# Another issue order for the mixers and the context feed-forward, and two more weight buffers for the small experts

## The chip, the cores and the metric

The kernel runs on one core of a Trainium2 chip. A core has a matrix engine (TensorE, PE in the rows), VectorE (DVE), ScalarE (ACT), GpSimd (POOL) and SyncE (SP), each with an instruction queue of its own that runs in order, and 16 DMA engines that serve the queues of all of them. The metric is the device time of one execution in microseconds, as the median of the runs.

## What is computed

Two transformer blocks stand one behind the other, on 256 tokens of width 1024, in float32. The first has two layers: a mixer (pooling, a gated convolution and spatial gating) and a feed-forward, which is dense in layer 0 and a mixture of experts in layer 1.

```python
for l in range(DEPTH):                                 # first block, DEPTH = 2
    mod = silu(c) @ ada_w[l] + ada_b[l]                # shift, scale and gate, two of each
    x = x + gate_m * (mixer1(rms_norm(x) * (1 + scale_m) + shift_m) @ w_out[l])
    h = rms_norm(x) * (1 + scale_f) + shift_f
    y = swiglu(h, ...) if l == 0 else moe_swiglu(h, ...)   # top 2 of 8 experts, hidden 3584
    x = x + gate_f * y
x = rms_norm(x, final_norm_g)
```

The second block takes this x and a context of 256 tokens. In its layer 0 the context goes through a mixer (a gated recurrence, differential attention, a Fourier mix) and a feed-forward of its own; neither needs x. In layer 1 only the context's keys and states are needed.

```python
for l in range(DEPTH):                                 # second block
    yl, yc = mixer(hl, hc, ...)                        # x also looks at the context's keys, states
    xl = xl + ml[2] * rms_norm_2(yl, g[1])
    xl = xl + ml[5] * rms_norm_2(swiglu_2(adaln(xl, ...), w_ffn_in[l], w_ffn_out[l]), g[3])
    if l < DEPTH - 1:                                  # the context stream, layer 0
        xc = xc + mc[2] * rms_norm_2(yc, g[1])
        xc = xc + mc[5] * rms_norm_2(swiglu_2(adaln(xc, ...), w_ffn_in[l], w_ffn_out[l]), g[3])
```

## The kernel before

Weights come in tiles of 128x1024 float32 (0.5 MB) by DMAs that SP issues (`wload`, line 213). In most layers each weight tile is split into a rounded part (ScalarE, line 320) and the remainder (VectorE, line 321), and each product is made of three matmuls (`mm3`, lines 236, 241 and 242). The small experts (the four with at most 64 tokens each) take the weights unsplit instead: a step loads four tiles and issues 16 products (`burst`, lines 260 and 264). The four large experts work as the other layers do.

The work is written as Python generators. A `Task` wraps one with a `Res`, the set of buffer pools that it takes its tiles from, and a key. A key is a priority class: `use` (line 135) sets the priority counter that each traced instruction gets, and the classes start at 0 (lead), one million (fill), two million (tail) and three million (late). When the kernel is built, a planner goes through the traced instructions with a timeline of its own, and puts on each engine, of the instructions that it takes to be ready, the one with the lowest number. So a lower class fills what a higher one leaves free; what is planned then runs in order on each engine.

`plan` (from line 1220) sets the classes. In the first block, `block1_mix` and `block1_ffn` of layer 0 and `block1_mix` of layer 1 are lead on resources R0 (tiles w0, h0, accumulators a0, t0). The context stream B with the modulation vectors G1 and G2 is fill on R1 (w1, w2, h1, h2, accumulators a1, t1, t2); for its feed-forward B goes to RF, which has three w1 and two h1 buffers, thus one split weight tile at a time. `block1_out` of layer 1 and `moe` are tail.

B runs as fill up to "normed", the point ahead of its feed-forward. That has 66 loads and as many steps, one load each: a gate/up step has 24 matmuls of 256 columns, a down step 12 of 512. Three of them are late. Then `moe` goes a step (normalization, router, and a branch at line 909 that only an overflow of the experts takes, which every engine reads a register for) and a second one (rows of the first expert). After it `turns` takes a's (expert steps) and b's (context steps) by a pattern; `issue_after` ties the first matmul of each to the last of the other before it. A small expert has 21 steps, so there are 84. When the small experts are through ("alone"), `moe` changes to RN, which also has the w1, w2, h1 and h2 buffers, and to a class below all others.

The weights of an expert are addressed by its number, which comes out of the routing, so no expert load can be issued before that. At its end the context stream adds a gate row that GpSimd loads (`gate_bc`, line 1318), multiplied in by VectorE at line 1344. In the small experts' resources RS, the weight tiles come in turn from w0 (four buffers) and h0 (four buffers).

Of the kernel before, what the change touches and what calls it, by code (L numbers as in the profile page):

```python
# [26 lines left out]
LEVELS = [64, 32, 16, 8, 4, 2, 1]  # L27
N_EXP = 8
LB_LAYER = 1
WEAVE = ("rardy" * 9, "r" + "arrdy" * 9)  # L30
W_BUFS, H_BUFS, S_BUFS = (4, 3, 1), (4, 2, 1), (12, 21, 6, 8)
K_BUFS, G_BUFS, M_BUFS, A_BUFS, T_BUFS = (4, 3), (3, 3), (8, 5), (2, 2), (2, 1, 1)
# [31 lines left out]
class Res:  # L64


    def __init__(self, w, h, a, aw, e, sc, t, s, st, sa, sb, k, g, m):
        self.w, self.h, self.a, self.aw, self.e, self.sc, self.t = w, h, a, aw, e, sc, t
        self.s, self.st, self.sa, self.sb, self.k, self.g, self.m = s, st, sa, sb, k, g, m
        self.sl = st  # L70
        self.i = {}
# [25 lines left out]
class Builder:  # L97
    def __init__(self, tc, A, out, es, taps=None):
        self.tc, self.nc, self.A, self.out = tc, tc.nc, A, out
        self.taps = taps or {}  # L100
        E = es.enter_context

        def pool(name, bufs, **kw):
            return E(tc.tile_pool(name=name, bufs=bufs, **kw))
        self.cp = pool("cp", 1)
        self.xp = pool("xp", 8)
        self.dp = pool("dp", 1, space=bass.MemoryType.DRAM)
        w = [pool(f"w{i}", n) for i, n in enumerate(W_BUFS)]
        h = [pool(f"h{i}", n) for i, n in enumerate(H_BUFS)]
        sp = [pool(f"s{i}", n) for i, n in enumerate(S_BUFS)]  # L110
        k = [pool(f"k{i}", n) for i, n in enumerate(K_BUFS)]
        g = [pool(f"g{i}", n) for i, n in enumerate(G_BUFS)]
        m = [pool(f"m{i}", n) for i, n in enumerate(M_BUFS)]
        a = [pool(f"a{i}", n, space=bass.MemoryType.PSUM) for i, n in enumerate(A_BUFS)]
        pt = [pool(f"t{i}", n, space=bass.MemoryType.PSUM) for i, n in enumerate(T_BUFS)]
        a0, a1, t0, t1, t2 = [a[0]], [a[1]], [pt[0]], [pt[1]], [pt[2]]
        s0, s1, s2, s3 = sp
        wl, hl = [w[0], w[1]] * 3 + [w[0], w[2]], [h[0], h[1]] * 2 + [h[0], h[2], h[0]]
        w1, h1, hm = [w[1]] * 3 + [w[2]], [h[1]] * 2 + [h[2]], [h[0], h[0], w[2]] + [h[0], h[0], h[2]]
        self.R0 = Res(w[:1], h[:1], a0, a0, a0, a0, t0, s0, s0, s2, s0, k[0], g[0], m[0])  # L120
        self.R1 = Res(w1, h1, a1, a1, a1, a1, t1 + t2, s1, s3, s1, s1, k[1], g[1], m[1])
        self.RF = Res(w[1:2], h[1:2], a1, a1, a1, a1, t1, s1, s1, s1, s1, k[1], g[1], m[1])
        self.RS = Res([w[0], h[0]], h[:1], t0, a0, a0, a0, t2 + a0, s3, s2, s2, s3, k[0], g[0], m[0])
        self.RM = Res(w[:1], hm, t0, a0, a0, a0, t2, s3, s2, s2, s3, k[0], g[0], m[0])
        self.RN = Res(wl, hl, t0 + a1, a0, a0, a0, t2 + t1, s3, s2, s2, s3, k[0], g[0], m[0])
        self.RL = Res(wl, hl, a0, a0 + a1, a1, t1 + t2, t0, s1, s0, s2, s3, k[0], g[0], m[0])
        self.R1.sl = s1
        self.xpools = [s0, s1]
        self.R = self.R0
        self.n = 0  # L130
        self.mark = None
        self.key = None
        self.prio = {"lead": 0, "fill": 1000000, "tail": 2000000, "late": 3000000}
# [1086 lines left out]
    def plan(self, xs, m, m2, sh, task, G0, G1, G2, G3):  # L1220
        R0, R1, RL = self.R0, self.R1, self.RL

        def weave(t, *others, label="end"):

            while t.at != label and t.step() != label:
                for o, n in others:
                    o.step(n)

        G0.step(4)
        G0.res = R0  # L1230
        G2.step(4)
        self.use(R1, "fill")
        self.levels_setup()
        if LB_LAYER == 1:
            self.lower_bounds()
        B = task(self.ctx_stream(m2, sh), R1, "fill")
        for _ in range(8):
            B.step()
            G2.step()
        weave(B, (G2, 1), (G1, 1), label="ffn")  # L1240
        G1.run()
        G2.run()
        B.res = self.RF

        weave(task(self.block1_mix(xs, m[0], 0), R0), (G0, 1))
        G0.run()
        task(self.block1_out(xs, m[0], 0), R0).run()
        task(self.block1_ffn(xs, m[0]), R0).run()
        task(self.block1_mix(xs, m[1], 1), R0).run()
        task(self.block1_out(xs, m[1], 1), R0, "tail").run()  # L1250
        moe = task(self.moe(xs, m[1]), self.RS, "tail")
        B.run("normed")
        B.key = "late"
        B.step(3)
        moe.step()
        moe.key = B.key = "tail"
        moe.step()
        self.turns(moe, B, "bbbbb" + "abaab" * 200)
        assert B.at == "end" and moe.at == "alone"
        self.prio["lead"] = 4000000  # L1260
        moe.key = "lead"
        moe.res = self.RN
        moe.run()
        self.use(RL, "lead")
        self.first_end(xs)
        self.tapx("x1", xs)
        self.tapx("xc", self.xc)
        L0 = task(self.lat_stream(xs, m2[0], 0, sh[0]), RL)
        weave(L0, (G3, 1), label="mixed")
        G3.run()  # L1270
        C = task(self.ctx_keys(m2, sh), R1)
        L0.run("ffn")
        L0.res = R0
        weave(L0, (C, 1))
        C.run()
        self.use(RL, "lead")
        self.tapx("xl0", xs)
        L1 = task(self.lat_stream(xs, m2[1], 1, sh[1]), RL)
        L1.run()
# [126 lines left out]
    def mixer2(self, l, H, sh, M, kind):  # L1406
# [77 lines left out]
        def ev_z(d):  # L1484
            lb = []

            def ev(t, ps):
                if l == LB_LAYER and t == 0:
                    lb.append(self.st(512))
                    self.late(nc.gpsimd.dma_start(lb[0], self.lb_rows[d:d + 1].to_broadcast([P, 512])))  # L1490
                    om = self.st(512)
                    S.activation(om, lb[0], AF.Copy, scale=-1.0, bias=1.0)
                    lb.append(om)
                k, f = self.st(512), self.s2(512, pool=self.R.sl)
                S.activation(k, ps, AF.Sigmoid, scale=-1.0)
                S.activation(f, ps, AF.Sigmoid)
                if lb:
                    V.tensor_mul(k, k, lb[1])
                    V.tensor_mul(f, f, lb[1])
                    V.scalar_tensor_tensor(f, f, 2.0 ** -64, lb[0], op0=ALU.max, op1=ALU.add)  # L1500
                    logs.append((f, None))
                else:
                    z = self.st(512)
                    V.tensor_scalar(z, ps, 0.0, None, op0=ALU.min)
                    V.tensor_tensor(f, f, k, op=ALU.min)
                    logs.append((f, z))
                lf[d].append(f)
                kt[d].append(k)
                if full:
                    pk = self.transpose4(k, 4)  # L1510
                    y = self.s2(4, 128)
                    S.copy(y, pk)
                    kT[d].append(y)
# [61 lines left out]
        if lat:  # L1575
# [15 lines left out]
            out = None  # L1591
            for c in WEAVE[l]:
                if c == "a":
# [478 lines left out]
```

## Time and profile before

| | us |
|---|---|
| median of 3 runs | 2841.42 |
| lowest and highest | 2837.86, 2845.29 |
| the profiled execution, its own time | 2833.26 |
| its span | 2831.5 |

| engine | busy us | share of the span |
|---|---|---|
| PE | 2620.4 | 93% |
| DVE | 1594.2 | 56% |
| ACT | 1323.8 | 47% |
| POOL | 104.7 | 4% |

Matmuls are pipelined, so a busy PE need not be a PE at its peak; an idle one is time in which no matmul was under way. The DMA share is the mean busy share of the 16 engines. A row of the timeline has the start, the duration, engine, line, operation, written and read tiles and the count; in brackets, the idle time of the engine before it and what ended it.

### The profile page before, as it was taken

The numbers are of one execution on the slowest core, as the hardware profiler recorded it, in microseconds if no ns is written. First come the engines' busy times: TensorE is split into PE (matmuls) and PEld (weight loads), VectorE is DVE, ScalarE is ACT, GpSimd is POOL, SyncE is SP. The second block draws the span as 40 slices with busy tenths as digits, with TensorE's granted clock in tenths as the row PEclk, the third lists the DMA queues.
The fourth block names the chain that finished last, engine by engine and source line by source line (L and its number), as shares of the span: only waits on it lengthen the run. The fifth ranks groups of instructions, "written<-read, shape, count | busy, mean of one in ns | idle before, by whom it ended". The sixth has DMA issues, their size and how long they took to land.

```text
span 2831.5 us, 44132 instructions
## 1 busy us (share of the span) xinstructions
PE 2620.4 (93%) x16414; PEld 1984.8 (70%) x16414; DVE 1594.2 (56%) x2691; ACT 1323.8 (47%) x1908; POOL 104.7 (4%) x166
## 2 busy tenths in 40 slices
PE   7899999998789899998899999989999999899898
PEld 5667888786654444444588787867768888677897
DVE  3436565665621222122699899985666556666555
ACT  3435445645322111111477777765545644554443
POOL 0010000010100000000000000000000000000000
PEclk8999999999899999999999999999999999899999
DMA  9987766643479999999799999986455556224463
GB/s 359 335 282 252 239 228 223 223 121 116 124 272 372 358 372 365 382 366 377 262 382 357 358 356 361 354 318 214 159 174 162 175 175 197 91 69 142 149 187 110
DMA packets 204383, 716.03 MB, mean 253 GB/s; under 512 B 24858, under 2 KB 29082, under 8 KB 204160
## 3 DMA queue, kind: packets, MB, share of 16 engines
q1 hardware_dynamic: 196112, 692.82, 69.8%
q0 software_dynamic: 7760, 19.75, 2.3%
q8 instruction: 131, 2.15, 0.3%
q14 instruction: 92, 0.75, 0.1%
q10 hardware_dynamic: 288, 0.55, 0.1%
HBM read 707.90 MB, written 5.13 MB: 252 GB/s over the span
## 4 chain that ended last, share of the span: by engine, by line
PE 55%; DMA 9%; DVE 3%; ACT 3%; issue 2%; SPq 0%; POOL 0%; DVEq 0%; ACTq 0%; POOLq 0%
PE a0t L236 7%; PE a0t L241 6%; PE a0t L242 6%; DMA h0t<-in_mgu_dram 6%; PE a1t L236 5%; PE a1t L241 5%; PE a1t L242 5%; PE t0t L264 4%; PE t0t L241 2%; PE t0t L242 2%; PE t0t L236 2%; PE t0t L260 2%; PE a0t L264 1%; PE a1t L1705 1%; DVE h0t L321 1%
## 5 line engine op out<-in xcount | busy, mean ns | idle before, releaser
L320 ACT CAST h0t<-w0t 128x1024 fp32r<-128x1024 f32 (+1 forms) x316 | 327.7, 1038 | 303.8 <-PE a0t L241 222.9
L321 DVE TENSOR_TENSOR h0t<-w0t,h0t 128x1024 fp32r<-128x1024 f32 (+1 forms) x214 | 257.2, 1203 | 230.0 <-ACT h0t L320 217.7
L320 ACT CAST h1t<-w1t 128x1024 fp32r<-128x1024 f32 x144 | 151.0, 1048 | 268.4 <-PE a1t L241 224.3
L236 PE MATMUL a0t<-s0t,h0t 128*128 128x256 f32 x800 | 226.6, 288 | 5.9 <-ACT h0t L320 2.9
L241 PE MATMUL a0t<-s0t,h0t 128*128 128x256 f32 x800 | 224.6, 284 | 0.0
L242 PE MATMUL a0t<-s0t,h0t 128*128 128x256 f32 x800 | 220.0, 286 | 0.2 <-DVE h0t L321 0.2
L321 DVE TENSOR_TENSOR h1t<-w1t,h1t 128x1024 fp32r<-128x1024 f32 x80 | 97.9, 1223 | 211.3 <-ACT h1t L320 207.1
L264 PE MATMUL t0t<-h0t,s0t 128*64 128x512 f32 x448 | 214.7, 625 | 0.0
L236 PEld LDWEIGHTS a0t<-s0t,h0t 128*128 128x128 f32 x800 | 153.0, 192 | 15.3 <-ACT h0t L320 4.6
L264 PE MATMUL t0t<-w0t,s0t 128*64 128x512 f32 x336 | 161.2, 618 | 0.0
L241 PEld LDWEIGHTS a0t<-s0t,h0t 128*128 128x128 f32 x800 | 153.7, 192 | 1.7 <-issue 1.1
L242 PEld LDWEIGHTS a0t<-s0t,h0t 128*128 128x128 f32 x800 | 150.1, 192 | 3.7 <-DVE h0t L321 1.7
L241 PE MATMUL a0t<-h0t,s2t 128*128 128x512 f32 x352 | 139.6, 397 | 0.0
L320 ACT CAST h0t<-w1t 128x1024 fp32r<-128x1024 f32 x101 | 106.1, 1051 | 45.4 <-PE a1t L242 17.1
L236 PE MATMUL a1t<-s1t,h1t 128*128 128x256 f32 x408 | 120.2, 298 | 5.4 <-ACT h1t L320 5.2
L242 PE MATMUL a0t<-h0t,s2t 128*128 128x512 f32 x308 | 120.0, 392 | 0.0
L264 PEld LDWEIGHTS t0t<-w0t,s0t 128*64 128x64 f32 x336 | 48.3, 144 | 99.6 <-issue 99.6
L241 PE MATMUL a1t<-s1t,h1t 128*128 128x256 f32 x408 | 116.0, 287 | 0.0
L236 PE MATMUL a0t<-h0t,s2t 128*128 128x512 f32 x308 | 113.0, 400 | 1.2 <-DVE s0t L1368 0.8
L242 PE MATMUL a1t<-s1t,h1t 128*128 128x256 f32 x396 | 110.6, 290 | 3.1 <-DVE h1t L321 3.1
L260 PE MATMUL t0t<-w0t,s0t 128*64 128x512 f32 x112 | 62.4, 640 | 46.8 <-DMA h0t<-in_mgu_dram 37.1
L236 PEld LDWEIGHTS a1t<-s1t,h1t 128*128 128x128 f32 x408 | 79.3, 195 | 36.3 <-issue 29.6
(804 smaller groups left out, 6770.1 us busy)
## 6 DMA issues: line engine op xcount, KB each, us to landing
w0t<-in_mgu_dram SPq DMA_DIRECT2D x224, 512.0 KB, 5.8
h0t<-in_mgu_dram SPq DMA_DIRECT2D x112, 512.0 KB, 9.2
w0t<-in_mdn_dram SPq DMA_DIRECT2D x112, 512.0 KB, 5.1
w1t<-in_mgu_dram SPq DMA_DIRECT2D x84, 512.0 KB
w0t<-in_f2gu_dram SPq DMA_DIRECT2D x66, 512.0 KB, 4.0
w1t<-in_f2gu_dram SPq DMA_DIRECT2D x61, 512.0 KB, 6.7
h0t<-in_mdn_dram SPq DMA_DIRECT2D x56, 512.0 KB, 7.1
w1t<-in_win_dram SPq DMA_DIRECT2D x54, 512.0 KB, 4.3
```

What stands on the lines that cost most here:

```text
L236: i = mm(ps, lh, rh, start=start if skip else first, stop=False, skip_group_check=skip)
L241: mm(ps, lh, rl, start=False, stop=False, skip_group_check=skip)
L242: self.last = mm(ps, ll, rh, start=False, stop=last, skip_group_check=skip)
L260: i = self.nc.tensor.matmul(*first[0], **first[1])
L264: self.last = self.nc.tensor.matmul(*a, **kw)
L320: self.nc.scalar.copy(out_h, src)
L321: self.nc.vector.tensor_sub(out_l, src, out_h)
L1705: nc.tensor.matmul(pe[:, h].rearrange("p a b -> p (a b)"), x[:, (h0 + h) * 128:(h0 + h + 1) * 128], rhs, start=i == 0, stop=i == 1)
```

## The change

The feed-forward of layer 0 and the mixer of layer 1 of the first block are tail instead of lead, so that fill (the context mixer, G1 and G2) has priority over them. Of the context feed-forward, 15 steps instead of three are late, and two instead of five go ahead of the small experts' first step. The small experts' resources have w2 and h2 (one buffer each) beside w0 and h0: ten weight tiles in the ring, not eight. No computation is added or taken away.

```diff
+PRE = 15
-        self.RS = Res([w[0], h[0]], h[:1], t0, a0, a0, a0, t2 + a0, s3, s2, s2, s3, k[0], g[0], m[0])
+        self.RS = Res([w[0], h[0]] * 4 + [w[2], h[2]], h[:1], t0, a0, a0, a0, t2 + a0, s3, s2, s2, s3, k[0], g[0], m[0])
...
         task(self.block1_out(xs, m[0], 0), R0).run()
-        task(self.block1_ffn(xs, m[0]), R0).run()
-        task(self.block1_mix(xs, m[1], 1), R0).run()
+        task(self.block1_ffn(xs, m[0]), R0, "tail").run()
+        task(self.block1_mix(xs, m[1], 1), R0, "tail").run()
         task(self.block1_out(xs, m[1], 1), R0, "tail").run()
         moe = task(self.moe(xs, m[1]), self.RS, "tail")
         B.run("normed")
         B.key = "late"
-        B.step(3)
+        B.step(PRE)
         moe.step()
         moe.key = B.key = "tail"
         moe.step()
-        self.turns(moe, B, "bbbbb" + "abaab" * 200)
+        self.turns(moe, B, "bb" + "abaab" * 200)
```

## Rows read from the trace of the kernel before

**Rows 1.** The page: span, TensorE's busy time, and tenths in 40 slices.

```profile
span 2831.5 us, 44132 instructions
PE 2620.4 (93%) x16414; PEld 1984.8 (70%) x16414; DVE 1594.2 (56%) x2691; ACT 1323.8 (47%) x1908; POOL 104.7 (4%) x166
PE   7899999998789899998899999989999999899898
DMA  9987766643479999999799999986455556224463
```

**Rows 2.** Stretches: length, busy PE, PEld, DVE, ACT, POOL (count), PEclk, DMA, GB/s.

```profile
215.00:536.00 321.00, 317.23 (x2427) 259.11 (x2428) 189.29 (x304) 166.42 (x233) 9.98 (x24) 0.99 0.72 236
536.00:745.00 209.00, 194.07 (x1336) 162.96 (x1335) 130.25 (x324) 104.02 (x161) 19.18 (x27) 0.98 0.44 135
745.00:771.50 26.50, 10.89 (x60) 9.75 (x58) 15.23 (x63) 8.55 (x18) 2.17 (x4) 0.71 0.22 65
771.50:809.60 38.10, 29.76 (x190) 26.37 (x192) 12.23 (x20) 12.69 (x17) 2.27 (x2) 0.89 0.65 214
809.60:1358.00 548.40, 497.35 (x2532) 254.80 (x2530) 115.99 (x163) 93.31 (x139) 9.84 (x8) 0.98 0.98 367
1358.00:1393.00 35.00, 25.58 (x84) 13.20 (x81) 16.93 (x27) 9.56 (x16) 1.12 (x2) 0.83 0.55 192
```

**Rows 3.** Stretches, matmuls into the context's accumulators a1t alone.

```profile
536.00:745.00 209.00, 76.90 (x402) 0.98 0.44 135
745.00:771.50 26.50, 5.37 (x31) 0.71 0.22 65
```

**Rows 4.** Timeline of SP's queue around the first expert's loads.

```profile
735.32 12.15 SPq L213 DMA_DIRECT2D w1t<-in_f2gu_dram  x3
...
771.68 0.36 SPq L213 DMA_DIRECT2D w0t<-in_mgu_dram  x1
...
780.04 26.25 SPq L213 DMA_DIRECT2D w1t<-in_f2gu_dram  x6
```

**Rows 5.** Timeline of PE: two neighbouring matmuls of a context gate/up step.

```profile
784.09 0.28 PE L236 MATMUL a1t<-s1t,h1t 128*128 128x256 f32 x1
784.21 0.28 PE L241 MATMUL a1t<-s1t,h1t 128*128 128x256 f32 x1
```

**Rows 6.** Timeline of VectorE: the remainders of two context weight tiles, one behind the other.

```profile
778.79 1.23 DVE L321 TENSOR_TENSOR h1t<-w1t,h1t 128x1024 fp32r<-128x1024 f32 x1 [3.92 <-ACT h1t L320]
...
783.73 1.23 DVE L321 TENSOR_TENSOR h1t<-w1t,h1t 128x1024 fp32r<-128x1024 f32 x1 [3.11 <-ACT h1t L320]
```

**Rows 7.** Timeline: PE after the branch, first expert's rows (ACT), its first product.

```profile
771.39 0.77 PE L934 MATMUL a0t<-cwt,s3t 128*128 128x2 f32 x3 [4.73 <-PEq L909]
...
788.54 0.58 ACT L1051 COPY s0t<-t2t 128x512 f32<-128x512 f32 x1
...
808.57 0.64 PE L260 MATMUL t0t<-w0t,s0t 128*64 128x512 f32 x1
```

**Rows 8.** DMA issues from 771.5 to 1393 us: the context feed-forward's.

```profile
w1t<-in_f2gu_dram SPq DMA_DIRECT2D x40, 512.0 KB, 6.8
w1t<-in_f2dn_dram SPq DMA_DIRECT2D x22, 512.0 KB, 7.8
```

**Rows 9.** Timeline at the turn to the large experts: GpSimd, VectorE, PE.

```profile
1382.47 0.55 POOL L1318 DMA_DIRECT2D s1t<-dt  x1 [6.38 <-PE a1t L236]
...
1388.93 0.69 DVE L1344 TENSOR_TENSOR s1t<-s1t,s1t 128x512 f32<-128x512 f32 x1 [2.95 <-DMA s1t<-dt]
...
1391.09 0.79 PE L241 MATMUL t0t<-h1t,s0t 128*128 128x512 f32 x1 [3.70 <-DVE h1t L321]
```

**Rows 10.** Stretches as in rows 2: the small experts' best 50 us.

```profile
1300.00:1350.00 50.00, 44.89 (x235) 22.82 (x232) 10.32 (x14) 8.56 (x14) 2.59 (x2) 1.00 1.01 390
```

**Rows 11.** Timeline of ScalarE: two function tables in turn (Silu, then Exp).

```profile
662.38 1.28 ACT L689 ACT_TABLE_LOAD   x1
...
667.26 1.28 ACT L1708 ACT_TABLE_LOAD   x1
```

## The prediction

> **What bounds the kernel now.** I read the page first. TensorE is busy for 93% of the span, so time is made or lost in the stretches where it is not, and in those where another resource is pegged [rows 1]. The slices show two such places: slices 10 and 11 (from 637 to 779 us), where the PE and DMA digits are both low, and the slices after 12, where the DMA digit is nearly always 9. I then cut the span by stage [rows 2]. From 215 to 536 us (first block's feed-forward, with the context mixer beside it) PE is busy 317.2 of 321.0 us: nothing to win. From 536 to 745 (second mixer, with the rest of the context mixer) it is idle 14.9 us, from 745 to 771.5 (end of routing) 15.6 of 26.5 us, while the DMA engines run at 135 and 65 GB/s. From 809.6 to 1358 (small experts) the DMA engines are 0.98 busy at 367 GB/s, and here the transfers set the time: a megabyte less is worth 2.7 us, and PE time is free as long as it fits (497 of 548 us busy). Two seams lie around that stage. Between 771.5 and 809.6 the rate is 214 GB/s, and between 1358 and 1393 it is 192.
>
> The queues say why. SP issues the first expert's loads at 771.7 us, then only six loads of the context feed-forward up to about 806 [rows 4]: the eight buffers of the small experts are full and nothing empties them, although the expert's gathered rows are ready from 788.5; its first product is issued at 808.6 [rows 7]. In between stand the steps of the context feed-forward that "bbbbb" puts ahead of it, one per 4.94 us [rows 6]. At the other seam, context steps that outlast the small experts wait for a gate row that GpSimd fetches at 1382.5; VectorE stands behind it, and with it the weight splits of the first large expert [rows 9].
>
> **The change part by part**, made against the profiled run (2833.3 us with the span of 2831.5), which lies 8.2 us under the median of the runs.
>
> 1. Twelve more context feed-forward steps go ahead of the routing (15 "late" steps for 3). A gate/up step is 24 matmuls, 0.12 us from start to start; 24 x 0.12 us is 2.9 us of PE [rows 5]. When only such steps run, they come 4.94 us apart, since two split buffers hold one step at a time [rows 6]. Before, the 31 a1t products from 745 to 771.5 make up some 1.3 steps [rows 3]. So 13.7 steps more, 13.7 x 2.9 = **+40 us** of PE ahead of the expert loads. Bounds: +40 if they interleave, 13.7 x 4.94 = +68 if they run alone. I take +40, since the second mixer and the routing run beside them.
>
> 2. The order of the mixers. The context mixer, still owing 76.9 us of a1t products at 536 us [rows 3], now goes ahead of the feed-forward of the first block, which is dense and fills its waits; behind that the second mixer and the routing keep their waits, and the late steps are there to fill them. On PE, SP, ScalarE, VectorE and GpSimd alike the feed-forward and its loads (from 215 us on) now queue behind context work; whoever waits for it (the second mixer, then the router) starts later by about those 77 us, and that much less competes with it afterwards. This part alone moves nothing in total, and DMA has room in that stretch (0.72 busy [rows 2]). What counts is the idle time: 3.8 + 14.9 + 15.6 = 34.3 us from 215 to 771.5 [rows 2]. The 4.7 us that PE stands at the branch of line 909 [rows 7] and a few more us of the router's short VectorE steps stay exposed. Recovered: between 0 (the second mixer's own waits are merely exposed at another place) and 34; I take two thirds, **-22 us**.
>
> 3. Fewer loads in the stage that DMA bounds. After 771.5 us 62 loads of the context feed-forward were still to be issued, 40 and 22 [rows 8]; of 66 that is all but four. With 15 steps done and three more loads in flight, 48 stay: 14 x 0.524 MB = 7.3 MB, at 367 GB/s **-20 us**. Bounds: 9 loads (the net move of steps, 17 for 8, ahead of the first expert) give -13; 14 give -20.
>
> 4. The seams. At 214 GB/s for 38.1 us, 38.1 x (1 - 214/367) = 15.9 us of transfer time are lost; with two steps instead of five ahead of the first expert, its first product can come some 18 us earlier, which is when its rows are there. At the other seam 35 x (1 - 192/367) = 16.7 us are lost; after the change 50 steps are woven at two to every three expert steps, so they end with 75 of the 84 expert steps, and the wait for the gate row falls where VectorE has time (116 of 548 us busy [rows 2]). Next late there is the first large expert's own splits, which no row shows without that wait. Of 32.6 us I take **-20**; bounds -8 (the second seam stays) and -30.
>
> 5. Ten weight buffers for eight. Two loads more, 1 MB or 2.9 us of transfer, start before the first product, and the ring rides out longer waits. The pools for it, w2 and h2, are not used by the context steps of this stage. With the engines 0.98 busy, the most that is left of 569 us of stage is 2%, 11 us. I take **-5**; bounds +3 (the ring's extra loads stand in front of a context load on SP) and -11.
>
> A rule that speaks for more: in the stage the engines reach 367 GB/s, and 390 GB/s at a busy share of 1.01 in the best 50 us [rows 10]. The Trainium skill's page "DMA: Bandwidth & Descriptors", section "Bandwidth", gives 425 GB/s as measured for one core with large transfers; by that rate the stage's 209 MB would take 491 us and not 569, and the sum would come out 78 us lower. No stretch of this trace runs at it.
>
> Sum: 40 - 22 - 20 - 20 - 5 = **-27 us**: 2833.3 - 27 = 2806 on the profiled run's scale, **2814 us** on that of the median.
>
> **The rivals.**
>
> A, slower: the late steps find no gaps. If the context mixer, held by its own three or four weight buffers, ends no earlier than the second mixer, the fifteen steps stand together behind it and run one per 4.94 us: +68, nothing recovered, against -20, -20 and -5. That is +23: **2864 us**. It decides once more than about 45 us are added ahead of the expert loads. For it: these steps did run at that pitch after 771.5 [rows 6]. Against: PE occupied 317 of 321 us while both streams were ready [rows 2], so either fills the other.
>
> B, no change: the idle time only moves. The second mixer without the context mixer beside it shows as much waiting as is filled elsewhere: +40 and 0 recovered, -20, -15, -5: **2841 us**. For it: the second mixer is a chain of short steps. Against: 15 dense steps are there for it.
>
> C, faster still: the deeper ring lifts the rate of the small experts to the 390 GB/s of the best window [rows 10]: 209 MB take 536 us for 569, 33 us less, of which 5 are counted: **2786 us**. Against: the busy share is 0.98 already.
>
> D, smaller gain: the recurrence's Exp now alternates with the feed-forward's Silu on ScalarE, and each change of table is a load of 1.28 us [rows 11]. Eleven Silu groups make up to 22 loads, 28 us; half of it on the chain gives +14: **2828 us**. Against: ScalarE is busy only 166 of 321 us there [rows 2]. The Trainium skill ("ScalarE: Activation LUTs", section "What ACT_TABLE_LOAD costs") has the same 1.28 us and a drain of 1.38 on top, and asks for calls grouped by table, which this order breaks; by its 2.66 us the 22 changes would be 59 us, half of them 29, and the time 2843.
>
> E, not done as written: order is the planner's, by priority among what it believes ready. If it places everything as before but for the first seam, only some -10 remain: **2831 us**.
>
> **How the numbers follow.** Forecast 0.52; A 0.13; B 0.15; C 0.08; D 0.07; E 0.05. The forecast's own range is 2797 to 2832. About 0.3% (8.5 us) is what a measurement of this kernel can tell from no change. The forecast, C and half of D and E, rounded up for the forecast's spread beyond its terms, give faster 0.67; B and the rest of D and E 0.18; A and a little of B 0.15. The range holds the forecast, D, E and B, and reaches to C and half of A: 2784 to 2852.
>
> **What would show it.** The expert loads start at 775 to 800 us, with PE idle under 15 us from 215 to there (step 2; over 30 is B). Eighteen context feed-forward loads are issued before them (step 3). The first expert's product follows its first load by about 20 us, not 37, and no wait for a gate row lies at the turn to the large experts (step 4). The small experts' rate stays near 367 GB/s (step 5; 390 is C). A large expert's stage of another length, or late steps 4.94 us apart ahead of the expert loads, would make the prediction wrong.

## The result and the profile after

The changed kernel takes 2766.9 us (median of four runs, 2765.6 to 2769.2) where the kernel before takes 2843.4 us on the same chip: a ratio of 0.9735, with a 95% interval from 0.9718 to 0.9752. It is 2.65% faster. The forecast was 2814 us with a range from 2784 to 2852: the direction was right, but the time lies below the range and the gain is nearly three times as large as forecast. The profiled execution took 2765.62 us.

The page of the profile after, with the lines that answer to [rows 1]:

```profile
span 2763.8 us, 44125 instructions
...
PE 2588.9 (94%) x16414; PEld 1972.0 (71%) x16414; DVE 1595.4 (58%) x2691; ACT 1317.0 (48%) x1903; POOL 103.6 (4%) x166
...
PE   7999999999979999998999999989999998998998
...
DMA  9987767345469999999999999975545565323563
```

The slices alone don't show where 67.7 us of span went: the DMA digits of the small experts are nearly all 9, as before. The stretches do (columns as in [rows 2]; the cuts follow the same events: end of the routing, first product, turn to the large experts):

```profile
215.00:799.50 584.50, 555.52 (x4141) 472.58 (x4139) 354.67 (x709) 294.89 (x432) 30.78 (x55) 0.98 0.59 192
...
799.50:812.70 13.20, 1.95 (x13) 1.52 (x13) 2.27 (x9) 0.59 (x1) 2.13 (x2) 0.57 0.87 288
812.70:1310.00 497.30, 472.42 (x2396) 234.31 (x2398) 116.74 (x182) 86.35 (x132) 9.70 (x10) 0.99 1.01 396
1310.00:1345.00 35.00, 32.44 (x139) 20.53 (x136) 24.53 (x30) 20.62 (x25) 0.00 (x0) 1.00 1.01 382
```

The small experts now get 396 GB/s, where they had 367 [rows 2]; the turn to the large experts runs at 382 with TensorE busy for 32.4 of 35 us, where it had 192 GB/s and 25.6 us. The timeline of the changed kernel gives the events (SP's queue, TensorE, GpSimd, TensorE):

```profile
775.73 18.30 SPq L214 DMA_DIRECT2D w1t<-in_f2gu_dram  x4
799.68 0.36 SPq L214 DMA_DIRECT2D w0t<-in_mgu_dram  x1
...
812.70 1.11 PE L261 MATMUL t0t<-w0t,s0t 128*64 128x512 f32 x1 [0.68 <-ACT s0t L1052]
...
1258.36 0.57 POOL L1319 DMA_DIRECT2D s1t<-dt  x1 [117.00 <-PE a1t L237]
...
1269.23 0.60 POOL L1319 DMA_DIRECT2D s1t<-dt  x1
...
1320.94 0.50 PE L237 MATMUL t0t<-h0t,s0t 128*128 128x512 f32 x1
```

The first expert's loads start at 799.7 us, 28.0 later than before [rows 4], with 20 loads of the context feed-forward ahead of them and not four. The first product follows 13.0 us later, not 36.9 [rows 7]. The gate rows are fetched at 1258 and 1269 us, inside the small experts, and no longer at the turn [rows 9].

From those events the span is cut into the same parts for every kernel that was run. "First load" is the first expert load; "to product" goes from there to the first small product; "small" from that to the first matmul of a large expert (1372.0 in the kernel before, after which it stands for the split that ends at [rows 9]'s last row; 1320.94 here); "large" from that to the first block's final normalization, whose first write is 1.9 us behind the last large expert's addition. GB/s is that of 830 to 1300 us (880 to 1350 in the late-only kernel). All of these are of the profiled executions, the ratio is that of the timed runs.

| kernel | first load | to product | small | large | GB/s | ratio, 95% interval |
|---|---|---|---|---|---|---|
| before | 771.7 | 36.9 | 563.4 | 521.5 | 367 | |
| changed | 799.7 | 13.0 | 508.2 | 505.7 | 398 | 0.9735 [0.9718, 0.9752] |
| changed, ring of eight | 801.4 | 12.8 | 560.8 | 505.7 | 362 | 0.9958 [0.9937, 0.9978] |
| before, ring of ten | 767.5 | 39.5 | 518.9 | 521.8 | 398 | 0.9834 [0.9815, 0.9853] |
| before, new priority | 784.0 | 12.6 | 559.0 | 520.6 | 370 | 0.9955 [0.9938, 0.9973] |
| before, late steps | 850.7 | 11.0 | 555.9 | 505.7 | 365 | 1.0111 [1.0076, 1.0146] |
| changed, ring of nine | 797.7 | 11.5 | 536.1 | 505.8 | 378 | 0.9804 [0.9765, 0.9843] |
| changed, ten tiles in another order | 802.9 | 12.6 | 516.2 | 505.6 | 390 | 0.9773 [0.9738, 0.9808] |
| before, priority and ring of ten | 782.8 | 13.5 | 516.0 | 518.2 | 401 | 0.9749 [0.9714, 0.9784] |
| ring of eight, no wait for all four | 801.5 | 12.2 | 521.3 | 504.0 | 389 | 0.9794 [0.9765, 0.9824] |
| ring of ten, no wait for all four | 800.4 | 12.1 | 501.3 | 503.9 | 405 | 0.9733 [0.9702, 0.9763] |
| nine late steps | 784.8 | 12.1 | 515.1 | 506.5 | 399 | 0.9744 [0.9714, 0.9775] |
| nine late steps, no wait for all four | 787.2 | 10.9 | 512.2 | 505.3 | 404 | 0.9710 [0.9686, 0.9734] |

The first two lines cut the difference: 28.0 - 23.9 - 55.2 - 15.8 us, and -0.8 behind them, together -67.7. The largest piece lies inside the small experts, where I had called the DMA engines full.

### The profile page after: what moved, and what is told of

Its sections match the earlier page's. It is cut to its first block, busy times and chain, and to the rows that moved or that the text cites. A ratio compares the mean times of both kernels' runs of the same rounds, so it can differ in the third digit from the quotient of the medians.

```text
span 2763.8 us, 44125 instructions
## 1 busy us (share of the span) xinstructions
PE 2588.9 (94%) x16414; PEld 1972.0 (71%) x16414; DVE 1595.4 (58%) x2691; ACT 1317.0 (48%) x1903; POOL 103.6 (4%) x166
## 4 chain that ended last, share of the span: by engine, by line
PE 60%; issue 11%; DMA 8%; DVE 4%; ACT 3%; POOL 0%; SPq 0%; DVEq 0%; ACTq 0%; POOLq 0%
PE a0t L237 7%; PE a0t L242 6%; PE a0t L243 6%; PE a1t L242 6%; PE a1t L237 6%; PE a1t L243 5%; PE t0t L265 4%; DMA h0t<-in_mgu_dram 3%; PE t0t L242 2%; PE t0t L237 2%; PE t0t L243 2%; PE a0t L265 2%; PE t0t L261 2%; PE a1t L1706 1%; PE t0t L1729 1%
## 5 line engine op out<-in xcount | busy, mean ns | idle before, releaser
L322 DVE TENSOR_TENSOR h0t<-w0t,h0t 128x1024 fp32r<-128x1024 f32 (+1 forms) x214 | 257.3, 1203 | 201.3 <-ACT h0t L321 183.2
L265 PE MATMUL t0t<-h0t,s0t 128*64 128x512 f32 x360 | 168.8, 607 | 0.0
L265 PE MATMUL t0t<-w0t,s0t 128*64 128x512 f32 x270 | 127.0, 600 | 0.0
L237 PE MATMUL a1t<-s1t,h1t 128*128 128x256 f32 x408 | 118.2, 293 | 4.5 <-ACT h1t L321 4.5
L242 PE MATMUL a1t<-s1t,h1t 128*128 128x256 f32 x408 | 114.5, 283 | 0.0
L243 PE MATMUL a1t<-s1t,h1t 128*128 128x256 f32 x396 | 108.4, 285 | 2.8 <-DVE h1t L322 2.8
L322 DVE TENSOR_TENSOR h1t<-w0t,h0t 128x1024 fp32r<-128x1024 f32 x68 | 83.1, 1222 | 33.6 <-ACT h0t L321 17.4
L242 PE MATMUL a1t<-h1t,s1t 128*128 128x512 f32 x240 | 96.2, 401 | 2.3 <-DVE h1t L322 2.2
```

What stands on the lines that cost most here:

```text
L237: i = mm(ps, lh, rh, start=start if skip else first, stop=False, skip_group_check=skip)
L242: mm(ps, lh, rl, start=False, stop=False, skip_group_check=skip)
L243: self.last = mm(ps, ll, rh, start=False, stop=last, skip_group_check=skip)
L265: self.last = self.nc.tensor.matmul(*a, **kw)
L322: self.nc.vector.tensor_sub(out_l, src, out_h)
```

## Where a busy share of 0.98 hid the time

The theory after the result: eight tiles did not keep the DMA engines fed, and a mean busy share of 0.98 does not show it. First two neighbouring loads of SP's queue in the kernel before, then single microseconds from 956 us (columns as above, the last two DMA share and GB/s):

```profile
949.77 0.33 SPq L213 DMA_DIRECT2D h0t<-in_mgu_dram  x1
955.75 0.34 SPq L213 DMA_DIRECT2D w1t<-in_f2dn_dram  x1
```

```profile
956.00:957.00 1.00, 1.00 (x8) 0.43 (x6) 0.92 (x2) 0.00 (x0) 0.00 (x0) 1.00 0.72 152
957.00:958.00 1.00, 1.00 (x8) 0.14 (x2) 0.00 (x0) 0.00 (x0) 0.00 (x0) 1.00 0.70 201
...
960.00:961.00 1.00, 1.00 (x9) 1.00 (x9) 0.69 (x1) 0.00 (x0) 0.00 (x0) 1.00 1.01 250
...
965.00:966.00 1.00, 1.00 (x6) 0.14 (x2) 0.00 (x0) 0.00 (x0) 0.00 (x0) 1.00 0.70 156
...
968.00:969.00 1.00, 1.00 (x7) 0.35 (x5) 0.00 (x0) 0.00 (x0) 0.00 (x0) 1.00 1.00 410
969.00:970.00 1.00, 1.00 (x7) 0.19 (x3) 0.00 (x0) 0.00 (x0) 0.00 (x0) 1.00 1.05 418
```

For 6 us no load is issued. When fed, the engines move 410 GB/s or more at a share of 1.00 to 1.05. When they run dry, the share falls only to 0.70 while the rate falls to 152 to 201, and a microsecond at 1.01 can move 250. So a share of 0.98 at 367 GB/s was 10% under a rate that the same stretch reached in 129 of the 470 microseconds from 830 to 1300.

The trace's DMA packets show both halves of this. Counted as bytes issued by SP less bytes of ended packets, 3.3 loads are under way on average from 830 to 1300 us in the kernel before and 4.3 in the changed one; fewer than two are for 13% and 3% of the time. And a 4 KB packet mostly takes 159 ns (16 engines with such packets end to end move 412 GB/s), but some take far longer, up to 1.3 us at 960 us, and count as busy all that time: packets over 300 ns are 3.2% before and 0.7% after. They also come with three or more loads under way, where the kernel before moves 374 GB/s and the changed one 400. That they go with the small ring is shown; what makes a packet long is not.

The rivals to this theory: that fewer context loads made the stretch shorter (my step 3), or that the new order did.

## The experiments

**The changed kernel with a ring of eight.**

```diff
-        self.RS = Res([w[0], h[0]] * 4 + [w[2], h[2]], h[:1], ...
+        self.RS = Res([w[0], h[0]], h[:1], ...
```

> The changed kernel with the small experts' ring of eight buffers as before; the new order stays. Theory 'ring': the two added weight buffers lifted the rate of the small experts from 367 to about 398 GB/s, worth 500 us at 367 against 398, some 40 us; so this kernel takes 2800 to 2815 us and its small experts run at 362 to 374 GB/s. Theory 'order': the gain comes from the order (fewer context loads in that stage, both seams gone, waits filled) and the buffers give at most the 11 us that the DMA engines' busy share of 0.98 leaves; so 2767 to 2780 us, with 388 GB/s or more.

Measured: 2823.2 us, ratio 0.9958. That is 8 us above the range of the theory 'ring' (and far above that of 'order'), at a rate within it. With everything else changed, the small experts take 560.8 us, 2.6 less than before, though ten context loads fewer are issued in that stretch (45 for 55). The two tiles are worth 52.6 us of that stretch; all the rest of the change is worth 0.4%.

**The kernel before with a ring of ten, and nothing else.**

```diff
-        self.RS = Res([w[0], h[0]], h[:1], ...
+        self.RS = Res([w[0], h[0]] * 4 + [w[2], h[2]], h[:1], ...
```

> The kernel before with the ring of ten as its only edit. Theory 'ring': the small experts run at 390 GB/s or more and the time is 2795 to 2815 us. Theory 'order': 367 to 375 GB/s and 2832 to 2843 us. If the two parts only help together, it stays within 10 us of before while the ring of eight in the new order also loses most of the gain.

Measured: 2786.7 us, ratio 0.9834; the stretch goes from 563.4 to 518.9 us at 398 GB/s, and both seams stay (39.5 us to the first product, 521.8 for the large experts). The gain is larger than the theory 'ring' had it, and it needs none of the other parts.

**The kernel before with the new priority alone.**

```diff
-        task(self.block1_ffn(xs, m[0]), R0).run()
-        task(self.block1_mix(xs, m[1], 1), R0).run()
+        task(self.block1_ffn(xs, m[0]), R0, "tail").run()
+        task(self.block1_mix(xs, m[1], 1), R0, "tail").run()
```

> The kernel before with the feed-forward of layer 0 and the second mixer set to tail, nothing else: three late steps, five steps ahead of the first expert, ring of eight. Theory 'waits filled': the waits of the context mixer are filled by the feed-forward, 22 of the 34 us of idle TensorE before the expert loads go, which then start at about 750 us and not 771.5; 2815 to 2828 us. Theory 'waits move': the second mixer shows the same idle time alone; the expert loads start at 765 to 778 us; 2835 to 2850 us.

Measured: 2823.7 us, ratio 0.9955. The first expert's loads start 12.3 us later, with 12 context loads ahead of them for four, and the first product follows after 12.6 us and not 36.9: the first seam closes with the five steps still in the pattern: twelve context loads are out by then. The second seam stays (520.6). The time lies in the range of 'waits filled', but not by that: TensorE is idle for 36.6 us from 215 us to the first expert load, where it was idle for 34.3.

**The kernel before with fifteen late steps, two ahead of the first expert.**

```diff
-        B.step(3)
+        B.step(15)
...
-        self.turns(moe, B, "bbbbb" + "abaab" * 200)
+        self.turns(moe, B, "bb" + "abaab" * 200)
```

> The kernel before with 15 late steps and two ahead of the first expert; the first block keeps its priority and the ring has eight. The late steps can't start before the context mixer ends, at about 730 us. If they find no waits there, they come 4.94 us apart, and the expert loads start at 810 to 840 us; the fewer loads and the two seams give back some 45 to 55 us: 2840 to 2865 us. If the routing's waits hide most of them, the loads start by 800 us and it takes 2815 to 2835 us.

Measured: 2863.8 us, ratio 1.0111: slower, by the mechanism of my rival A. Its stretches ahead of the expert loads, and VectorE's splits of two context tiles in a row:

```profile
743.00:770.00 27.00, 15.14 (x86) 13.57 (x85) 18.56 (x77) 9.18 (x20) 0.00 (x0) 0.75 0.18 55
770.00:800.00 30.00, 22.50 (x128) 20.28 (x128) 8.11 (x9) 8.87 (x10) 0.00 (x0) 0.80 0.32 96
800.00:851.00 51.00, 34.25 (x173) 27.47 (x172) 14.51 (x21) 12.77 (x15) 2.17 (x4) 0.87 0.35 105
```

```profile
812.52 1.23 DVE L321 TENSOR_TENSOR h1t<-w1t,h1t 128x1024 fp32r<-128x1024 f32 x1 [3.10 <-ACT h1t L320]
817.44 1.23 DVE L321 TENSOR_TENSOR h1t<-w1t,h1t 128x1024 fp32r<-128x1024 f32 x1 [3.69 <-ACT h1t L320]
```

The late steps stand alone behind the routing, 4.92 us apart, at 96 to 105 GB/s and with TensorE idle for 16.8 of 51 us. The first expert load moves by 79.0 us for 14 more context loads (4 to 18), to 850.7 us where 840 was the latest expected. With the new priority the twelve late steps cost 17.4 us (784.0 with the priority alone, 801.4 in the ring-of-eight kernel) for eight more loads. And 505.7 us for the large experts shows what closes the second seam: fewer context steps in the pattern, whatever the ring.

**A ring of nine**, to see whether the gain comes by degrees:

```diff
-        self.RS = Res([w[0], h[0]] * 4 + [w[2], h[2]], h[:1], ...
+        self.RS = Res([w[0], h[0]] * 4 + [w[2]], h[:1], ...
```

> The changed kernel with a ring of nine (w2 added, h2 not). A step takes four tiles and what is left of the ring is what can be in flight meanwhile: four of eight, five of nine, six of ten. Theory 'depth': the gain of 56 us from eight to ten (2823 to 2767) comes in two like parts or mostly with the first; 2780 to 2800 us, small experts at 380 to 390 GB/s. Rival 'whole steps': the ring helps only where half a step more fits (ten); then within 8 us of the ring of eight, 2815 us or more.

Measured: 2788.0 us; the stretch takes 536.1 us at 378 GB/s, between 560.8 with eight and 508.2 with ten. It comes by degrees, 25 and 28 us a tile.

**Ten tiles, two of which come round after eight loads.**

```diff
-        self.RS = Res([w[0], h[0]] * 4 + [w[2], h[2]], h[:1], ...
+        self.RS = Res([w[0], h[0]] * 3 + [w[2], h[2]], h[:1], ...
```

> The changed kernel with the ring [w0, h0] three times, then w2, h2: the same ten buffers, but w2 and h2 come again after eight loads, so at that point of each round only eight loads can be under way. Theory 'depth': no better than the ring of eight, 2810 to 2830 us. Rival 'more buffers of any kind': most of the gain stays, 2765 to 2785 us.

Measured: 2779.3 us, 516.2 us at 390 GB/s. Inconclusive as a split of the number of tiles from their order: w2 and h2 come again after eight loads, while w0 and h0, four of each for three turns, may run further ahead.

**The kernel before with the priority and the ring of ten**: three late steps and "bbbbb" kept, the edits of the second and third experiments together.

> The priority change and the ring of ten, but three late steps and five ahead of the first expert as before. With a ring of eight the late steps brought nothing beside the priority change (2823 and 2824 us). Theory 'steps ahead are an even trade' (2.9 us of TensorE each ahead of the expert loads, a like time saved in the stage): 2763 to 2775 us. Theory 'the late steps need the faster stage to pay': 2780 us or more, so that they are worth 10 us or more of the change.

Measured: 2770.6 us, ratio 0.9749, whose interval holds the changed kernel's. Against the changed kernel the expert loads start 16.9 us earlier, the small experts take 7.8 us longer and the large ones 12.5 us longer: the late steps are an even trade, as far as can be measured.

**The small experts alone, ring of eight**: the ring edit of the first experiment, and the context steps are all put behind the small experts.

```diff
-        self.turns(moe, B, "bb" + "abaab" * 200)
+        self.turns(moe, B, "bb" + "a" * 90 + "b" * 200)
```

> The changed kernel with the ring of eight and no context step woven into the small experts: after the first two all the rest comes behind the last small expert, one by one. No work is left out. Theory 'the context step drains the ring' (while it runs, nothing frees expert tiles, and four loads in flight last 5.1 us against 3.4 + 2.9 us): without it the small experts run at 395 GB/s or more even with eight. Rival 'eight tiles can't hold the rate': 360 to 375 GB/s as with the context steps. Total time is of no interest: some 47 steps at 4.94 us stand alone, so about 2900 us or more.

Measured: 3016.5 us in one run (the context feed-forward, then alone, makes it so long). What counts is the stretch from 830 to 1300 us, with no context step in it:

```profile
830.00:1300.00 470.00, 344.97 (x1382) 114.68 (x1378) 26.47 (x73) 22.58 (x58) 7.32 (x8) 0.92 0.96 354
```

TensorE is idle for 125 of 470 us, and still only 354 GB/s come, less than either theory had. So the context steps, their loads in SP's queue and their matmuls are not needed to drain the ring; eight tiles don't hold the rate even alone. What remains is the expert step itself. One of them in the ring-of-eight kernel, SP's queue and TensorE:

```profile
1000.01 0.33 SPq L214 DMA_DIRECT2D w0t<-in_mgu_dram  x1
...
1002.30 0.86 SPq L214 DMA_DIRECT2D h0t<-in_mgu_dram  x1
...
1008.48 0.45 SPq L214 DMA_DIRECT2D h0t<-in_mgu_dram  x1
...
1011.16 0.61 PE L261 MATMUL t0t<-w0t,s0t 128*64 128x512 f32 x1 [2.34 <-DMA h0t<-in_mgu_dram]
...
1014.12 0.33 SPq L214 DMA_DIRECT2D w0t<-in_mdn_dram  x1
```

The four loads of the step that starts at 1011.16 are issued from 1000.01 to 1002.30. The last of them is in the chain of work that ended last, with its time to landing:

```profile
1002.30 8.72 DMA h0t<-in_mgu_dram
```

The step's first product waits for it, by a dependence that `burst` makes ("products in one go"), though the other three had landed at 1007.22, 1008.50 and 1009.76 by the trace's landing events. Meanwhile SP issues the next step's loads; at 1008.48 all eight tiles are taken, and none is free until the waiting step uses up its first ones, at 1014.12: 5.6 us in which no load is issued. The microseconds around it:

```profile
1011.00:1012.00 1.00, 0.84 (x4) 0.40 (x6) 0.00 (x0) 0.00 (x0) 0.00 (x0) 0.94 1.03 385
1012.00:1013.00 1.00, 1.00 (x4) 0.30 (x2) 0.00 (x0) 0.00 (x0) 0.00 (x0) 0.50 1.04 401
1013.00:1014.00 1.00, 1.00 (x6) 0.42 (x4) 0.00 (x0) 0.00 (x0) 0.00 (x0) 0.50 1.01 397
1014.00:1015.00 1.00, 1.00 (x6) 0.45 (x4) 0.00 (x0) 0.00 (x0) 0.00 (x0) 0.50 0.82 336
1015.00:1016.00 1.00, 1.00 (x7) 0.21 (x3) 0.00 (x0) 0.00 (x0) 0.00 (x0) 0.85 0.88 184
1016.00:1018.00 2.00, 2.00 (x11) 1.30 (x8) 0.00 (x0) 0.00 (x0) 0.00 (x0) 1.00 0.99 401
```

**That dependence taken away, ring of eight.** If tiles come free late because of it, eight should nearly do.

```diff
-        self.tc.add_manual_dep(i.ins, self.loaded.ins.name, LATE, reason="products in one go")
...
-        self.RS = Res([w[0], h[0]] * 4 + [w[2], h[2]], h[:1], ...
+        self.RS = Res([w[0], h[0]], h[:1], ...
```

> The changed kernel with a ring of eight, and without the dependence that holds the first product of a small expert's step until all four loads of that step have landed. Theory (eight tiles are too few because a step frees its tiles late and in a burst: it waits for its last load while the tiles of its first three lie idle): the products follow each load, tiles come free earlier, the small-expert stretch goes from 361 GB/s to 380 GB/s or more, and the time from 2823 us to 2780 to 2805 us. Rival (eight tiles in flight are too few however they are freed): 355 to 368 GB/s and 2815 to 2835 us. A second rival (products that follow each load let a late load hold TensorE in the middle of a step, and the context's matmuls stand behind it): 2840 us or more.

Measured: 2778.0 us, ratio 0.9794, where the ring of eight with the wait has 0.9958. Each product still waits for its own tile. The waits of TensorE and of SP's queue from 820 to 1300 us (us in total, times, longest), with the wait and without, both with eight tiles:

```profile
PE t0t L261 <- DMA h0t<-in_mgu_dram: 38.7, 23, 4.0
...
SPq L214 <- PE t0t L265: 135.3, 85, 6.8
SPq L214 <- DVE h1t L322: 80.1, 18, 5.6
```

```profile
PE t0t L264 <- DMA h0t<-in_mgu_dram: 3.3, 5, 1.8
...
SPq L214 <- PE t0t L264: 176.9, 121, 4.4
...
SPq L214 <- DVE h1t L321: 12.5, 3, 4.6
...
830.00:1300.00 470.00, 463.89 (x2254) 225.23 (x2253) 114.83 (x179) 82.78 (x127) 9.03 (x10) 1.00 1.00 389
```

389 GB/s with eight tiles, for 362, and the stretch is 39.5 us shorter. TensorE's wait for the fourth load goes from 38.7 to 3.3 us, and SP's wait at context loads, whose tile is held by a split that waits in turn for context matmuls, from 80.1 to 12.5. SP's wait for the products to free a tile does not fall, it grows (135.3 to 176.9 us); what changes is how much is under way meanwhile: 4.1 loads on average where it was 3.2, and fewer than two for 5% of the time where it was 14%. So the late freeing is shown as a cause. How much of the gain is its own depends on the order: of the 43 GB/s between the ring of eight with the wait (362) and the ring of ten without (405), dropping the wait makes 27 if it comes first and 7 if the two tiles come first, which then make 36. The two remedies overlap. And TensorE's wait for loads and SP's wait for tiles are one loop, which no run cut apart.

**The same with the ring of ten.**

> The changed kernel, ring of ten, without the dependence that holds the first product of a small expert's step until all four of its loads have landed. If late freeing is still what keeps the stretch at 396 GB/s and not at the 410 that its best microseconds show, the rate rises by 5 to 12 GB/s and the time is 2750 to 2762 us. If ten tiles already cover it: 2763 to 2771 us, as the changed kernel. If holding TensorE in the middle of a step costs more: 2772 us or more.

Measured: 2763.4 us, ratio 0.9733: the same as the changed kernel, as far as can be told. The stretch gets 405 GB/s and is 6.9 us shorter, and SP's queue waits for other things:

```profile
SPq L214 <- PE t0t L264: 57.3, 52, 4.4
SPq L214 <- DMA h0t<-in_mgu_dram: 46.5, 65, 1.4
SPq L214 <- DMA w0t<-in_mgu_dram: 41.2, 57, 2.1
...
830.00:1300.00 470.00, 465.46 (x2303) 226.42 (x2303) 115.33 (x180) 82.84 (x128) 9.67 (x10) 1.00 1.03 405
```

SP now waits mostly for an earlier load to land (199 us in all) and less for matmuls to free a tile (89 us). That load is always the one eight before on the queue: the loads take turns at eight semaphores, so not more than eight are under way whatever the ring. On average 5.0 are. Here the transfers are near the pace that they can keep. TensorE, busy for 465.5 of 470 us, has little left either.

**Nine late steps for fifteen** (`PRE = 9`).

> The changed kernel with nine late context steps where it has fifteen. The prediction has each further late step as an even trade (about 2.9 us of TensorE ahead of the first expert's loads, paid back by the load that no longer stands among the experts' and by filled gaps): by the runs with three late steps (2771 us) and with fifteen (2767 us), 2763 to 2772 us, with the first expert's loads 7 to 12 us earlier than in the changed kernel and the stretch of the small experts longer by as much. If late steps cost more than they give: under 2760 us. If the last gap (between the small and the large experts) closes only with fifteen: 2772 to 2785 us.

Measured: 2762.9 us, ratio 0.9744: the expert loads start 14.9 us earlier and the small experts take 6.9 us longer; the difference to the changed kernel is within what can be measured, and the turn to the large experts stays closed (506.5).

**Both last edits together**: no wait for all four, nine late steps.

> The changed kernel without the dependence that holds a step's first product until all four loads have landed, and with nine late context steps where it has fifteen: the two edits that each gave some 4 us less than the changed kernel, within what can be measured. If their gains are real and come at different places (the rate of the small experts; the time of the first expert's loads), 2752 to 2760 us. If both were chance: 2763 to 2770 us. If nine late steps leave more context loads for a stretch that is now bound by bytes, each taking 0.5 MB at 404 GB/s, the earlier start is paid back in full: 2760 to 2767 us.

Measured: 2757.7 us (six runs, 2757.1 to 2764.6), ratio 0.9710 [0.9686, 0.9734]. It has the lowest time of all the kernels, but its interval still overlaps the changed kernel's, so it is not shown to be faster.

## Why the prediction was wrong, point by point

**Steps 1 and 2** (+40 and -22, net +18; measured +28.0). Twenty context loads are ahead of the expert loads, as against 18 foreseen. TensorE's work from 215 us to there grew by 33.3 us (522.2 to 555.5), near the 40. But its idle time went from 34.3 to 29.0 us only: 5 recovered, not 22. The step put the test itself: under 15 us idle would be right, over 30 rival B. It came out nearly as B, and with the priority alone (36.6 us) as B: the idle time moved. The end of the routing is filled, but idle time opened in the first block's feed-forward. Two stretches of the changed kernel (TensorE idle for 10.2 and 1.6 us, where [rows 2] has 3.8 and 15.6):

```profile
215.00:536.00 321.00, 310.79 (x2461) 257.97 (x2460) 183.26 (x316) 170.99 (x247) 11.59 (x22) 0.99 0.67 224
...
745.00:771.50 26.50, 24.92 (x163) 22.56 (x163) 16.95 (x35) 11.13 (x18) 1.07 (x2) 1.00 0.31 92
```

Without the priority, rival A is real (+79.0 us, 4.92 us apart, where I had +68 and 4.94). Only its condition failed: under the new priority the late steps did find the second mixer beside them.

**Step 3** (-20) failed as reasoned. From the first expert load to the first matmul of a large expert 7.2 MB less are moved than before, as foreseen (7.3). But 4.2 MB of that left the wait ahead of the first product (seven context loads stood there, not the six that I had counted), where the engines had room and which step 4 charges as well; the stretch itself moved 204.3 MB and moves 201.3 (202.1 with the ring of eight, where it is 2.6 us shorter). From the priority-and-ring kernel to the changed one 3.1 MB fewer gave 7.8 us, their time at the 396 GB/s of the stretch. The 1.43 us a load (0.524 MB at 367 GB/s) was not the error; charging it for loads that stood ahead of the stretch was.

**Step 4** (-20 of 32.6) was sized too small: -23.9 at the first seam and -15.8 at the second, where the full terms had 15.9 and 16.7. The first closes by either of two ways: by the priority with "bbbbb" kept (12.6 us), and by late steps and "bb" without the priority (11.0). What is left of it, 13.0 us, is mostly the wait for the expert's rows (TensorE's, in two pieces between the first load and the first product):

```profile
PE t2t L1050 <- DMA s3t<-dt,m0t: 10.5, 2, 6.2
```

The second is as worked out: the last gate row at 1269 us is (1269 - 812.7) / 508.2 = 0.90 of the stretch, with 74 of the 84 expert steps begun where 75 were foreseen. Steps 3 and 4 together were -40, and -42.5 with the ring of eight (-2.6, -24.1, -15.8): two errors that nearly cancel.

**Step 5** (-5, bounds +3 and -11) is the step that failed, by 47.6 us: -52.6 in the new order, -44.5 in the old. I read a busy share of 0.98 as 2% left. In its place the runs showed a ring that drains: 3.3 loads under way with eight tiles, 4.3 with ten, and 367 GB/s going to 398. The numbers against it were in the trace of before: 390 GB/s at 1.01 in [rows 10] is 6% more rate for 3% more share, and TensorE waits 37.1 us for h0t's loads at L260 from 809 to 1358 us. The bound of 11 was a ratio of shares where a ratio of rates was asked for. Rival C, at 0.08, had the mechanism; it stopped at 390 GB/s since no 50 us of the trace ran faster, and single microseconds at 410 were not looked at.

A rate of the Trainium skill stood against the step: "DMA: Bandwidth & Descriptors", section "Bandwidth", with its 425 GB/s measured for one core with a 16 MB transfer. No stretch measured here reaches it: the best has 405 GB/s, the changed kernel 396 to 398. But it pointed the right way against the 367 that I had taken for a ceiling.

**Rivals D and E.** Table loads of ScalarE from 215 to 800 us fell from 35 to 29, and ScalarE's count of instructions falls from 1908 to 1903. D is out. E is out as well: 20 loads stand where four did. The large experts' stage, apart from the turn, has its length within 1%: 505.7 us, where the kernel before takes 501.4 from the end of its stand (1392.1) on.

With the measured sizes the sum closes: from -27, with +10 (steps 1 and 2), -2.5 (3 and 4) and -47.6 (5), it comes to -67.1; measured are -67.7.

What stays open: how much of the ring's gain comes by the clock (below), what makes single packets long, and whether the waits of SP at context loads (80.1 us with eight tiles) cost anything of their own, which no run took away alone.

## What to carry to other kernels

A DMA share near one says that packets are under way, not that they move at full rate: compare the mean rate of the stretch with the best single microseconds in it, and count the loads under way. What the issuing queue waits for tells the two ends apart (only matmuls and splits at 362 GB/s, mostly earlier loads at 405), but not what lies between: in the changed kernel, at 398, SP still waits 201 us for matmuls and 44 for earlier loads. Where steps wait for all of their tiles before they use the first, count the ring in steps: eight tiles were two steps of four, and the ninth and the tenth tile gave 25 and 28 us; dropping the wait gave 39.5 of those 52.6 us without a byte of memory. Charge bytes at the rate only where they leave the stretch that the bytes pace.

## What the runs showed of the hardware

The rate over 470 us reached 405 GB/s at a share of 1.03, through loads of 0.5 MB issued from one queue; with drained queues the share said 0.96 to 0.98 at 354 to 367. Of the 4 KB packets, 3.2% took over 300 ns in the kernel before and 0.7% in the changed one, where the median is 159 to 161.

A short wait of TensorE has a second price. In the ring-of-eight step above, the granted clock is 1.00 until 1011 us; after the 2.34 us wait it is 0.94 in the first microsecond and 0.50 from 1012 to 1015 (the 1.2 GHz level of the two), and matmuls of one shape take longer there than a few microseconds later:

```profile
1012.17 1.06 PE L265 MATMUL t0t<-w0t,s0t 128*64 128x512 f32 x1
...
1015.45 0.59 PE L265 MATMUL t0t<-w0t,s0t 128*64 128x512 f32 x1
```

1.06 us against 0.59, just when their tiles should come free. The mean clock of 830 to 1300 us is 0.92 with the experts alone, 0.97 with the ring of eight and 1.00 in the changed kernel, so the drained ring and the lower clock come together; what the clock alone costs was not separated.
